# One decoder layer on one core: the branch, the masks, the gating and a modulation put elsewhere, and the first counts of two blocks held behind index sums

## The chip, the core and the metric

The kernel runs on one core of a Trainium2 chip. The metric is the device time of one execution in microseconds (us). Engines are named as the profile names them: PE (TensorE), PEld (its weight loads), DVE (VectorE), ACT (ScalarE), POOL (GpSimd), SP (SyncE).

## What is computed

One layer for 1024 positions of width 1024, in float32. The parts that this change touches, cut from the reference:

```python
# mixer A: spatial gating (4 groups of 128 channels, chunks of 128 positions)
z_u, z_v = gelu(p_u), gelu(p_v);  v = rms_norm(z_v per group)
out_A = u * (tril(W_s[g]) v_chunk + b[g])
# mixer B: sparse attention, 8 heads of 64; the indexer picks the 256 best keys of each query
dots  = einsum('bthd,bsd->bths', q_idx, k_idx) * IDX_DIM ** -0.5
score = einsum('bth,bths->bts', w * IDX_HEADS ** -0.5, relu(dots))      # causal
_, idx = top_k(score, 256)
o = softmax(q . k[idx] * HEAD_DIM ** -0.5) v[idx]
# then
x  = x + g1 * rms_norm(concat(rms_norm(out_A), rms_norm(o)) W_out)
h2 = rms_norm(x) * (1 + scale2) + shift2
x  = x + g2 * rms_norm(relu(h2 W_1)^2 W_2)
```

## The kernel before

The 1024 positions are eight blocks of 128 rows; block b has 128(b+1) causal keys, so only blocks 2 to 7 have keys to drop. A scheduler places all work: it walks the program in priority order (the order of the code, or a number set in `tc.cur_priority`), and fixes for each engine one list of instructions, which the engine then runs strictly in order. Semaphores between engines follow from the tiles; a tile with one buffer makes its users take turns.

The stages around the change:

- **Indexer (stage 3)**, blocks 7, 6, 5, 4, 3, 2. For each of 8 heads PE multiplies (L449) into PSUM tiles `lg`, ACT evicts with a relu (L450) into one of two `relu` buffers, and DVE adds them up into `SC` (L452 for the first head, L454 for the other seven). `qs` (L391/L392) are the stacked queries of the products.
- **Gating (stage 4)**, 16 block halves. PE projects u and v (24 matmuls, L301/L303/L304), ACT does gelu (L517), two squares (L522) and two scalings (L527), PE the gating product (L531), DVE adds the bias and multiplies (L534), ACT squares the result (L536). All of it stands in one function, `gating`, which is called one projection later. Then q of eight blocks is projected (`q_proj`, 24 matmuls each, copied by ACT, L560): six before the selection, two more in `search_rest`.
- **Selection (stage 5)**, blocks 7 to 2. `select` counts the positive scores (`count`, L592), prepares a 16-bit key (L622 to L627), and finds the threshold in 15 rounds: on DVE (blocks 7, 5, 2: L599, L601, L603, scratch `spare`) or on ACT by Sign (blocks 6, 4, 3: L611, with L612 and L613 on DVE, scratch `spare2`); a tail (L633 to L642) follows. `spare` and `spare2` have one buffer each, so searches on one engine take turns.
- **The branch**: `search_rest` brings a count from DVE through a PE product (L648), a cast (L649) and a load of the value into DVE's control flow (L652), which decides whether a longer search is run. It is not run with these inputs.
- **Masks**: `mask` (L667 to L680, DVE) turns threshold and scores of a block into a bias of its logits. `mask(7)` follows `search_rest` at once, the others are spread over the attention loop.
- **Attention (stage 6)**, blocks in the order 0, 7, 1, 6, 5, 4, 3, 2, four units each. Per unit: logits on PE (L727), evicted by DVE with the bias and a running extreme (L728), Exp on ACT (L731), transposes and values on PE (L766, L752).
- **Second norm (stage 8)**: `h2_block` transposes on PE (L895) and ACT evicts with the modulation (L898), 64 pieces of 128x128.

The order of masks 6 to 2 in the attention loop is set by `MASKS`, unit number to block:

```python
    MASKS = {4: 6, 6: 5, 8: 4, 9: 3, 10: 2}
```

Of the kernel before, what the change touches and what calls it, by code (L numbers as in the profile page):

```python
# [9 lines left out]
F32 = mybir.dt.float32  # L10
F32R = mybir.dt.float32r
BF = mybir.dt.bfloat16
# [7 lines left out]
P = 128  # L20
# [17 lines left out]
def trunk(ctx, tc, x, c, positions, w_ada, b_ada, g_pre_mix, w_in, g_sgu_v, w_spatial, b_spatial,  # L38
# [8 lines left out]
    def nm(s):  # L47
        uid[0] += 1
        return f"{s}_{uid[0]}"
# [16 lines left out]
    def p_tr():  # L66
        return ps.tile([P, 512], F32, tag="tr", name=nm("tr"), bufs=3)
# [354 lines left out]
                        pattern=[[-1, P]], channel_multiplier=1)  # L422
    i_stack, ip = push("ip", "right")
    stage(3)
    spare = up.tile([P, 1024], BF, name="spare")
    wC0 = w_chunk(w_in, [(0, C_QI, 512)])
    QI = {}
    IB = (7, 6, 5, 4, 3, 2)
# [1 line left out]
    def qi_proj(b):  # L430
        p = p_mm()
        proj(p, b, wC0, 512)
        QI[b] = ip.tile([P, 512], F32, tag="qi", name=nm("qi"), bufs=2)
        A.activation(QI[b], p, AF.Copy)
        rope(QI[b], b, 8, kp)

    def index(b):
        n = P * (b + 1)
        sc = SC[:, soff[b]:soff[b] + n]
        ch = chunks(n)  # L440
        for grp in range(2):
            qs = q_stack(ip, QI[b], grp, ip.tile([P, 2, 512], F32R, tag="qs", name=nm("qs"), bufs=2))
            for h4 in range(4):
                h = grp * 4 + h4
                r = ip.tile([P, 1024], F32, tag="relu", name=nm("relu"), bufs=2)
                for c0, w in ch:
                    pl = p_lg()
                    for q in range(2):
                        T.matmul(pl[:, :w], qs[:, q, h4 * P:(h4 + 1) * P], KI[:, c0:c0 + w], start=q == 0, stop=q == 1)  # L449
                    A.activation(r[:, c0:c0 + w], pl[:, :w], AF.Relu)  # L450
                if h == 0:
                    V.tensor_scalar(sc, r[:, :n], WI[:, b, h:h + 1], None, op0=OP.mult)  # L452
                else:
                    V.scalar_tensor_tensor(sc, r[:, :n], WI[:, b, h:h + 1], sc, op0=OP.mult, op1=OP.add)  # L454
        G.affine_select(out=sc[:, n - P:], in_=sc[:, n - P:], compare_op=OP.is_ge, fill=NEG, base=0,
                        pattern=[[-1, P]], channel_multiplier=1)

# [54 lines left out]
    stage(4)  # L512
    ssv = ct([P, NB, 4], F32, "ssv")
    ssa = ct([P, NB, 2], F32, "ssa")
    def gating(cc, j, p):
        uv = up.tile([P, 512], F32, tag="uv", name=nm("uv"), bufs=2)
        ge = A.activation(uv, p, AF.Gelu_apprx_tanh)  # L517
        vn = up.tile([P, 2, P], F32, tag="vn", name=nm("vn"), bufs=2)
        ss = ssv[:, j, 2 * cc:2 * cc + 2]
        v = uv[:, 256:512]  # L520
        for i in range(2):
            A.activation(vn[:, i], v[:, i * P:(i + 1) * P], AF.Square, accum_out=ss[:, i:i + 1])  # L522
        G.tensor_tensor(v, v, gvb[:, 256 * cc:256 * cc + 256], op=OP.mult)
        G.tensor_scalar(ss, ss, 1.0 / P, EPS, op0=OP.mult, op1=OP.add)
        G.tensor_tensor(ss, ss, mhalf[:, :2], op=OP.pow)
        for i in range(2):
            A.activation(vn[:, i], v[:, i * P:(i + 1) * P], AF.Copy, scale=ss[:, i:i + 1])  # L527
        pg = p_tr()
        ya = up.tile([P, 2, P], F32, tag="ya", name=nm("ya"), bufs=2)
        for i in range(2):  # L530
            T.matmul(pg[:, i * P:(i + 1) * P], WM[:, 2 * cc + i], vn[:, i], start=True, stop=True)  # L531
        for i in range(2):
            g = 2 * cc + i
            V.scalar_tensor_tensor(ya[:, i], pg[:, i * P:(i + 1) * P], cols[:, 72 + g:73 + g],  # L534
                                   uv[:, i * P:(i + 1) * P], op0=OP.add, op1=OP.mult)
        A.activation(vn.rearrange("p a b -> p (a b)"), ya.rearrange("p a b -> p (a b)"), AF.Square,  # L536
                     accum_out=ssa[:, j, cc:cc + 1])
        nc.sync.dma_start(ya_dram[j * P:(j + 1) * P, 256 * cc:256 * cc + 256], ya.rearrange("p a b -> p (a b)"))
        return ge

    pend = []
    for cc in range(2):
        wt = w_chunk(w_in, [(0, C_U + 256 * cc, 256), (256, C_V + 256 * cc, 256)])
        for j in range(NB):
            p = p_mm()
            proj(p, j, wt, 512)
            pend.append((cc, j, p))
            if len(pend) > 1:
                gating(*pend.pop(0))


    wQ = w_chunk(w_in, [(0, C_Q, 512)])
# [7 lines left out]
        A.activation(QT[b], p, AF.Copy)  # L560
        rope(QT[b], b, 8, qp)

    for b in OB[:6]:
        q_proj(b)
        if pend:
            last_gelu = gating(*pend.pop(0))

# [5 lines left out]
        G.memset(nth[:, k:k + 1], float(k + 1))  # L575
    spare2 = up.tile([P, 7 * P], mybir.dt.int8, name="spare2")
    ON_ACT = (6, 4, 3)

    ST = {}
    KDS = ct([P, 6], F32, "kds")  # L580
# [8 lines left out]
        return SC[:, soff[b]:soff[b] + P * (b + 1)]  # L589

    def count(b, thr, dst):
        V.tensor_scalar(BI[:, boff[b]:boff[b] + P * (b + 1)], score(b), thr, None, op0=OP.is_ge, op1=OP.add, accum_out=dst)  # L592

    def search(u, top, tf, cnt, kd, kk, step=lambda: None):

# [20 lines left out]
    def select(b):  # L616
        n = P * (b + 1)
        cnt, sg, kk, tf, kq, lf, top8, kd, th, lo, hi = ST[b]
        sc = score(b)
        jb = BI[:, boff[b]:boff[b] + n]  # L620
        count(b, 0.0, cnt)
        V.tensor_scalar(sg, cnt, TOPK - 0.5, 2.0, op0=OP.is_ge, op1=OP.mult)  # L622
        V.tensor_scalar(sg, sg, 1.0, None, op0=OP.subtract)
        a = (2 * TOPK - 1 - n) / 2.0
        V.tensor_scalar(kd, sg, a, n - TOPK + 1 + a, op0=OP.mult, op1=OP.add)

        V.tensor_scalar(jb, sc.bitcast(BF).rearrange("p (n two) -> p n two", two=2)[:, :, 1], sg, None, op0=OP.mult)  # L627
        u = jb.bitcast(I16)
        if b in ON_ACT:
            search_signs(u, 14, tf, cnt, kd, kk, kq)  # L630
        else:
            search(u, 14, tf, cnt, kd, kk)
        V.tensor_copy(hi, tf)  # L633
        V.tensor_scalar(spare[:, :n], u, tf, None, op0=OP.is_gt, op1=OP.add, accum_out=cnt)
        V.tensor_tensor(kd, kd, cnt, op=OP.subtract)

        V.scalar_tensor_tensor(jb.bitcast(U16), u, tf, sc.bitcast(U16).rearrange("p (n two) -> p n two", two=2)[:, :, 0],
                               op0=OP.is_equal, op1=OP.mult)
        v = jb.bitcast(U16)
        V.max(out=top8, in_=v)  # L640
        V.tensor_scalar(pick, nth, kd, None, op0=OP.is_equal)
        V.tensor_tensor_reduce(pick, pick, top8, scale=1.0, scalar=0.0, op0=OP.mult, op1=OP.add, accum_out=lf)  # L642

    def search_rest():

        V.tensor_scalar(more[:, :6], KDS, 8.0, None, op0=OP.is_gt, op1=OP.add, accum_out=more[:, 6:7])
        p = p_tr()
        flag = T.matmul(p[:1, :1], more[:, 6:7], ones, start=True, stop=True)  # L648
        V.tensor_copy(rest, p[:1, :1])  # L649
        for b in OB[6:]:  # L650
            q_proj(b, flag)
        with tc.tile_critical():  # L652
            r = V.value_load(rest)
            with V.If(r > 0):
                for b in range(2, NB):
                    cnt, sg, kk, tf, kq, lf, top8, kd, th, lo, hi = ST[b]
                    search(BI[:, boff[b]:boff[b] + P * (b + 1)].bitcast(U16), 15, lf, cnt, kd, kk, V.drain)
                V.drain()

    masked = [None]  # L660

    def mask(b):

# [1 line left out]
        cnt, sg, kk, tf, kq, lf, top8, kd, th, lo, hi = ST[b]  # L665
        sc = score(b)
        first = V.tensor_copy(lo, lf)  # L667
        V.scalar_tensor_tensor(th, hi, 16, lo, op0=OP.logical_shift_left, op1=OP.bitwise_or)

        V.tensor_tensor(tf, th.bitcast(F32), sg, op=OP.mult)  # L670
        lt = BI[:, boff[b]:boff[b] + n]
        eq = up.tile([P, 1024], BF, tag="uv", name=nm("eq"), bufs=2)[:, :n]
        after(first, masked[0])
        V.tensor_scalar(lt, sc, tf, None, op0=OP.is_lt, op1=OP.add, accum_out=cnt)
        V.tensor_scalar(eq, sc, tf, BIG, op0=OP.is_equal, op1=OP.mult)
# [6 lines left out]
    for b, pri in PRI:  # L682
        tc.cur_priority = pri
        select(b)
    tc.cur_priority = 465000
    search_rest()
    mask(7)


    stage(6)  # L690
# [24 lines left out]
    def logits(u):  # L715
# [3 lines left out]
        for h2 in range(2):  # L719
# [4 lines left out]
            for i, (c0, cw) in enumerate(ch):  # L724
                pl = p_lg()[:, :cw]
                for q in range(2):
                    T.matmul(pl, QS[b, grp][:, q, h4 * P:(h4 + 1) * P], KS[:, grp, c0:c0 + cw], start=q == 0, stop=q == 1)  # L727
                V.tensor_tensor_reduce(L[:, c0:c0 + cw], pl, bias[:, c0:c0 + cw], scale=-0.125, scalar=top,  # L728
                                       op0=OP.add, op1=OP.min, accum_out=mxs[:, i, b, h:h + 1])
                top = mxs[:, i, b, h:h + 1]  # L730
            ex = A.activation(L, L, AF.Exp, scale=-1.0, bias=top, accum_out=sms[:, b, h:h + 1])  # L731
# [94 lines left out]
    logits(0)  # L826
    stack_for(2)
    for u, (b, grp, pair) in enumerate(units):
        if u + 1 < len(units):
            logits(u + 1)  # L830
        values(u)
# [52 lines left out]
    def h2_block(j, y):  # L884
# [5 lines left out]
        for half in range(2):  # L890
# [4 lines left out]
                T.transpose(p[:, i * P:(i + 1) * P], y[:, k * P:(k + 1) * P], ident)  # L895
            for i in range(4):
                k = half * 4 + i
                A.activation(f[:, k, :], p[:, i * P:(i + 1) * P], AF.Identity, scale=G2[:, k:k + 1],  # L898
                             bias=SH2[:, k:k + 1])
        tk = slice(t, t + P)  # L900
        if hh == 0:
            for half in range(2):
# [379 lines left out]
```

## Time and profile before

| what | value |
|---|---|
| runs | 1244.34, 1246.61, 1664.87 us; median 1246.61 |
| profiled execution | 1243.53 us, of which the span of the profile is 1241.8 (1.7 outside it) |
| PE busy | 1161.0 us, 93% of the span |
| DVE busy | 861.9 us, 69% |
| ACT busy | 680.6 us, 55% |
| POOL busy | 212.0 us, 17% |
| chain that ended last | PE 59%, DVE 6%, issue 3%, ACT 3%, DMA 2% |

Busy shares are averages over stages with different limits; what a change in one stage is worth is read in that stage. A timeline row gives start and duration, the engine, the line, the operation, output <- input, and in brackets how long the engine had been idle before it and what ended that.

### The profile page before, as it was taken

How to read it: one execution, taken by the hardware profiler on the slowest of the kernel's cores; microseconds unless marked ns; L12 is line 12 of the kernel's file. 1: busy time of each engine (PE TensorE's matmuls, PEld its weight loads, DVE VectorE, ACT ScalarE, POOL GpSimd, SP SyncE). 2: the span in 40 equal slices, each digit the busy share in tenths (PEclk: the TensorE clock that was granted, in tenths of full speed). 3: DMA queues.
4: the chain of work that ended last, by engine and by line, in shares of the span. 5: the costliest groups of instructions: out<-in, count | busy, mean ns of one | idle time of the engine just before them, and what ended most of it. 6: DMA issues, size and time to landing. Idle time of an engine off the chain costs nothing.

```text
span 1241.8 us, 16873 instructions
## 1 busy us (share of the span) xinstructions
PE 1161.0 (93%) x5785; PEld 979.4 (79%) x5785; DVE 861.9 (69%) x1766; ACT 680.6 (55%) x1442; POOL 212.0 (17%) x304
## 2 busy tenths in 40 slices
PE   4899969899698999899899999999999999999997
PEld 4887857688588998887777888888887888888886
DVE  6944998956697666626698775655548756876568
ACT  4554569681267755538925555555544554445452
POOL 3695503553300000022510000000000000000001
PEclk9899969899799999999999999999999999999999
DMA  9431100210002044446315853444458455533335
GB/s 345 150 93 35 52 1 18 86 47 31 1 10 69 26 162 162 179 157 215 103 51 186 297 171 127 170 138 150 161 210 340 136 186 178 196 91 96 102 101 204
DMA packets 80240, 162.42 MB, mean 131 GB/s; under 512 B 7724, under 2 KB 32920, under 8 KB 80152
## 3 DMA queue, kind: packets, MB, share of 16 engines
q1 hardware_dynamic: 80136, 161.33, 38.6%
q8 instruction: 45, 0.74, 0.2%
q14 instruction: 43, 0.35, 0.1%
q10 hardware_dynamic: 16, 0.00, 0.0%
HBM read 119.36 MB, written 41.94 MB: 130 GB/s over the span
## 4 chain that ended last, share of the span: by engine, by line
PE 59%; DVE 6%; issue 3%; ACT 3%; DMA 2%; POOL 0%; SPq 0%; DVEq 0%; POOLq 0%; ACTq 0%
PE tr L1162 8%; PE lg L1162 8%; PE mm L1162 5%; PE mm L752 4%; PE lg L980 3%; PE lg L981 3%; PE lg L979 3%; PE tr L981 3%; PE tr L980 3%; PE tr L979 3%; PE tr L766 2%; PE lg L727 2%; PE mm L981 2%; PE mm L980 2%; PE mm L979 2%
## 5 line engine op out<-in xcount | busy, mean ns | idle before, releaser
L872 ACT ACTIVATE w<-rx 128x512 fp32r<-128x512 f32 x112 | 70.6, 631 | 146.4 <-PE lg L1162 61.7
L1162 PE MATMUL tr<-w,w 128*128 128x512 f32 x504 | 133.4, 389 | 2.7 <-DVE w L873 2.7
L1162 PE MATMUL lg<-w,w 128*128 128x512 f32 x504 | 133.1, 389 | 0.0
L873 DVE TENSOR_TENSOR w<-rx,w 128x512 fp32r<-128x512 f32 x112 | 77.2, 689 | 57.5 <-ACT w L872 57.3
L301 PE MATMUL mm<-w,hT 128*128 128x512 f32 (+1 forms) x288 | 112.0, 390 | 4.4 <-ACT hT L293 3.7
L1162 PEld LDWEIGHTS tr<-w,w 128*128 128x128 f32 x504 | 94.5, 188 | 22.7 <-DVE w L873 3.1
L303 PE MATMUL mm<-w,hT 128*128 128x512 f32 (+1 forms) x288 | 111.3, 387 | 0.0
L304 PE MATMUL mm<-w,hT 128*128 128x512 f32 (+1 forms) x288 | 110.3, 384 | 0.4 <-POOL hT L294 0.4
L1162 PEld LDWEIGHTS lg<-w,w 128*128 128x128 f32 x504 | 94.6, 188 | 19.6
L1198 POOL TENSOR_TENSOR rsf<-rsf,mhalf 128x1 f32<-128x1 f32 x8 | 6.0, 750 | 602.5 <-DVE rsf L1197 602.5
L1162 PE MATMUL mm<-w,w 128*128 128x512 f32 x336 | 93.9, 389 | 0.0
L752 PEld LDWEIGHTS mm<-VV,pT 128*128 128x128 f32 x576 | 73.4, 194 | 4.9 <-ACT pT L747 2.9
L752 PE MATMUL mm<-VV,pT 128*128 128x64 f32 x576 | 74.7, 273 | 1.3 <-ACT pT L747 1.3
L1162 PEld LDWEIGHTS mm<-w,w 128*128 128x128 f32 x336 | 63.1, 188 | 13.1
L873 DVE TENSOR_TENSOR w<-b,w 128x512 fp32r<-128x512 f32 x96 | 65.7, 685 | 3.8 <-ACT w L872 3.8
L301 PEld LDWEIGHTS mm<-w,hT 128*128 128x128 f32 x288 | 55.2, 192 | 15.1 <-ACT hT L293 3.9
L873 DVE TENSOR_TENSOR w<-s,w 128x512 fp32r<-128x512 f32 x56 | 38.1, 689 | 37.4 <-ACT w L872 37.4
L727 PE MATMUL lg<-KS,qs 128*128 128x512 f32 (+5 forms) x192 | 51.4, 376 | 12.6 <-DVE qs L392 10.7
L872 ACT ACTIVATE w<-b 128x512 fp32r<-128x512 f32 x96 | 59.3, 618 | 6.5 <-DMA b<-in_w_ff_dram 6.5
L304 PEld LDWEIGHTS mm<-w,hT 128*128 128x128 f32 x288 | 54.9, 191 | 10.0 <-POOL hT L294 0.6
L303 PEld LDWEIGHTS mm<-w,hT 128*128 128x128 f32 x288 | 55.3, 192 | 8.5
L731 ACT ACTIVATE L<-L,mxs 128x128 f32<-128x128 f32 (+7 forms) x64 | 49.2, 770 | 22.9 <-DVE mxs L728 22.7
(355 smaller groups left out, 2975.5 us busy)
## 6 DMA issues: line engine op xcount, KB each, us to landing
rx<-x_scratch SPq DMA_DIRECT2D x56, 512.0 KB, 3.6
x_scratch<-d SPq DMA_DIRECT2D x108, 256.0 KB, 3.0
ada<-in_w_ada_dram SPq DMA_DIRECT2D x48, 512.0 KB, 5.6
raw<-in_w_ff_dram SPq DMA_DIRECT2D x32, 512.0 KB, 4.0
b<-in_w_ff_dram SPq DMA_DIRECT2D x32, 512.0 KB, 4.4
x<-in_x_dram SPq DMA_DIRECT2D x16, 512.0 KB, 5.4
raw<-in_w_in_dram SPq DMA_DIRECT2D x8, 512.0 KB, 3.8
raw<-in_w_in_dram SPq DMA_DIRECT2D x16, 256.0 KB, 2.8
```

Of the source, the lines that this page charges most:

```text
L301: mm = T.matmul(p[:, :n], lh, wt[k][:, 0, :n], start=k == 0, stop=False)
L303: T.matmul(p[:, :n], lh, wt[k][:, 1, :n], start=False, stop=False)
L304: T.matmul(p[:, :n], ll, wt[k][:, 0, :n], start=False, stop=k == KD - 1)
L727: T.matmul(pl, QS[b, grp][:, q, h4 * P:(h4 + 1) * P], KS[:, grp, c0:c0 + cw], start=q == 0, stop=q == 1)
L731: ex = A.activation(L, L, AF.Exp, scale=-1.0, bias=top, accum_out=sms[:, b, h:h + 1])
L752: mm = T.matmul(po[:, o:o + 64], e[:, (si * 2 + h2) * P:(si * 2 + h2 + 1) * P], VV[:, s0 + si, grp], start=first, stop=pair == 1 and s0 + ...
L872: A.activation(hi, src, AF.Copy)
L873: eng.tensor_tensor(lo, src, hi.bitcast(F32), op=OP.subtract)
L979: ms.append(T.matmul(p, a[:, 0, k], b[:, 0, k], start=start and k == 0, stop=False, skip_group_check=more))
L980: ms.append(T.matmul(p, a[:, 0, k], b[:, 1, k], start=False, stop=False, skip_group_check=more))
L981: ms.append(T.matmul(p, a[:, 1, k], b[:, 0, k], start=False, stop=stop and k == 3, skip_group_check=more))
L1162: ms.append(T.matmul(p, x[:, qa, t * P:(t + 1) * P], y[:, qb], start=start and n == 0, stop=stop and n == 2, skip_group_check=more))
```

## The change

Seven edits, the diff cut to its core:

```diff
-    spare = up.tile([P, 1024], BF, name="spare")
+    spare = up.tile([P, 1024], mybir.dt.int8, name="spare")
...
+    summed = {}
...
-                    V.scalar_tensor_tensor(sc, r[:, :n], WI[:, b, h:h + 1], sc, op0=OP.mult, op1=OP.add)
+                    summed[b] = V.scalar_tensor_tensor(sc, r[:, :n], WI[:, b, h:h + 1], sc, op0=OP.mult, op1=OP.add)
...
-    def gating(cc, j, p):
-        uv = up.tile([P, 512], F32, tag="uv", name=nm("uv"), bufs=2)
+    def gate_in(cc, j, p):
+
+        uv = up.tile([P, 512], F32, tag="uv", name=nm("uv"), bufs=3)
...
+        pend.append((cc, j, uv, vn))
+        return ge
+
+    def gate_out(cc, j, uv, vn):
+
         pg = p_tr()
-        ya = up.tile([P, 2, P], F32, tag="ya", name=nm("ya"), bufs=2)
+        ya = up.tile([P, 2, P], F32, tag="ya", name=nm("ya"), bufs=1)
...
-        A.activation(vn.rearrange("p a b -> p (a b)"), ya.rearrange("p a b -> p (a b)"), AF.Square,
-                     accum_out=ssa[:, j, cc:cc + 1])
+        A.activation(pg[:, :2 * P], ya.rearrange("p a b -> p (a b)"), AF.Square, accum_out=ssa[:, j, cc:cc + 1])
...
-            pend.append((cc, j, p))
             if len(pend) > 1:
-                gating(*pend.pop(0))
+                gate_out(*pend.pop(0))
+            last_gelu = gate_in(cc, j, p)
...
-    for b in OB[:6]:
+    for b in OB[:4]:
         q_proj(b)
         if pend:
-            last_gelu = gating(*pend.pop(0))
+            gate_out(*pend.pop(0))
...
+    BEHIND = {7: 6, 6: 5}
...
-        count(b, 0.0, cnt)
+        after(count(b, 0.0, cnt), summed[BEHIND.get(b, b)])
...
-        for b in OB[6:]:
+        for b in OB[4:]:
             q_proj(b, flag)
...
+        if b < 7:
+            after(first, lowest[0])
...
-        eq = up.tile([P, 1024], BF, tag="uv", name=nm("eq"), bufs=2)[:, :n]
+        eq = up.tile([P, 1024], BF, tag="uv", name=nm("eq"), bufs=3)[:, :n]
...
-    tc.cur_priority = 465000
-    search_rest()
-    mask(7)
...
-                V.tensor_tensor_reduce(L[:, c0:c0 + cw], pl, bias[:, c0:c0 + cw], scale=-0.125, scalar=top,
+                lowest[0] = V.tensor_tensor_reduce(L[:, c0:c0 + cw], pl, bias[:, c0:c0 + cw], scale=-0.125, scalar=top,
...
     for u, (b, grp, pair) in enumerate(units):
+        if u == 3:
+            at = tc.cur_priority
+            tc.cur_priority = 465000
+            search_rest()
+            mask(7)
+            tc.cur_priority = at
...
-                A.activation(f[:, k, :], p[:, i * P:(i + 1) * P], AF.Identity, scale=G2[:, k:k + 1],
-                             bias=SH2[:, k:k + 1])
+                g, sh = G2[:, k:k + 1], SH2[:, k:k + 1]
+                if half == 0:
+                    A.activation(f[:, k, :], p[:, i * P:(i + 1) * P], AF.Identity, scale=g, bias=sh)
+                else:
+                    V.tensor_scalar(f[:, k, :], p[:, i * P:(i + 1) * P], g, sh, op0=OP.mult, op1=OP.add)
```

In words: (1) the first count of block 7 stands behind the last index sum of block 6, that of block 6 behind the last sum of block 5. (2) `gating` is split: gelu, squares and scaling right behind their own projection, the product and what follows one projection later; `uv` has three buffers, `ya` one, and the square of `ya` goes to PSUM. (3) Four q projections stand ahead of the selection, four in `search_rest`. (4) `search_rest` and `mask(7)` are emitted in the attention loop behind block 0's first units. (5) Masks of blocks below 7 stand behind the last logits eviction emitted. (6) `spare` holds 8-bit integers. (7) Half of the 64 modulations go from ACT to DVE. Behind the change lines shift by 2 to 17: L592 is L600, L599 L608, L611 L620, L627 L636, L648 L657, L728 L736.

Where DVE's list has the first count of block 7 (`self_2716` before, `self_2650` in the changed kernel; 128x1024 is block 7, 128x896 block 6). Before:

```order
L392 TENSOR_TENSOR qs_1221<-tr_1224,qs_1221 128x512
L592 TENSOR_SCALAR BI,self_2716<-SC 128x1024
L452 TENSOR_SCALAR SC<-relu_1181,WI 128x896
L622 TENSOR_SCALAR self_2716<-self_2716 128x1
L454 SCALAR_TENSOR_TENSOR SC<-relu_1191,WI,SC 128x896
L623 TENSOR_SCALAR self_2716<-self_2716 128x1
L625 TENSOR_SCALAR kds<-self_2716 128x1
L627 TENSOR_SCALAR BI<-SC,self_2716 128x1024
L454 SCALAR_TENSOR_TENSOR SC<-relu_1201,WI,SC 128x896
L599 TENSOR_SCALAR spare,self_2716<-BI,self_2716 128x1024
```

In the changed kernel:

```order
L456 SCALAR_TENSOR_TENSOR SC<-relu_1231,WI,SC 128x896
L456 SCALAR_TENSOR_TENSOR SC<-relu_1241,WI,SC 128x896
L456 SCALAR_TENSOR_TENSOR SC<-relu_1251,WI,SC 128x896
L456 SCALAR_TENSOR_TENSOR SC<-relu_1261,WI,SC 128x896
L600 TENSOR_SCALAR BI,self_2650<-SC 128x1024
L392 TENSOR_TENSOR qs_1357<-tr_1360,qs_1357 128x512
L631 TENSOR_SCALAR self_2650<-self_2650 128x1
L632 TENSOR_SCALAR self_2650<-self_2650 128x1
L634 TENSOR_SCALAR kds<-self_2650 128x1
L636 TENSOR_SCALAR BI<-SC,self_2650 128x1024
L454 TENSOR_SCALAR SC<-relu_1317,WI 128x768
L608 TENSOR_SCALAR spare,self_2650<-BI,self_2650 128x1024
```

The count and the first round (L599, L608) of block 7 stood among the first sums of block 6 (`relu_1181` and on); now all eight sums of block 6 are ahead of them, and the rounds stand among the sums of block 5 (`relu_1317` and on).

Where ACT's list has the first Sign of block 6 (`self_2714` before, `self_2648` in the changed kernel; relus of 128x384 belong to block 5, of 128x320 to block 4). Before:

```order
L391 ACTIVATE qs_1357<-tr_1360 128x512
L450 ACTIVATE relu_1317<-lg_1318 128x384
L450 ACTIVATE relu_1317<-lg_1322 128x384
L450 ACTIVATE relu_1327<-lg_1328 128x384
L611 ACTIVATE spare_2701,self_2714<-BI,self_2714 128x896
L450 ACTIVATE relu_1327<-lg_1332 128x384
L611 ACTIVATE spare_2701,self_2714<-BI,self_2714 128x896
```

In the changed kernel:

```order
L391 ACTIVATE qs_1546<-tr_1549 128x512
L452 ACTIVATE relu_1483<-lg_1484 128x320
L452 ACTIVATE relu_1483<-lg_1488 128x320
L452 ACTIVATE relu_1503<-lg_1504 128x320
L452 ACTIVATE relu_1503<-lg_1508 128x320
L620 ACTIVATE spare_2635,self_2648<-BI,self_2648 128x896
L452 ACTIVATE relu_1513<-lg_1514 128x320
L452 ACTIVATE relu_1513<-lg_1518 128x320
```

It stood among the relus of block 5's second head; now it stands behind those of block 4's fifth head.

Where PE's list has the flag of the branch (`ones,more`), with projections of q behind it (`mm`) and logits of blocks 0 and 7 (`lg`, 128x128 and 128x512). Before:

```order
L304 MATMUL mm_2659<-w_2470,hT_143 128x512
L301 MATMUL mm_2659<-w_2473,hT_143 128x512
L303 MATMUL mm_2659<-w_2473,hT_143 128x512
L304 MATMUL mm_2659<-w_2473,hT_143 128x512
L648 MATMUL tr_3073<-ones,more 1x1
L301 MATMUL mm_3076<-w_2446,hT_142 128x512
L303 MATMUL mm_3076<-w_2446,hT_142 128x512
```

In the changed kernel:

```order
L760 MATMUL mm_3056<-VV,pT_3079 128x64 x2
L735 MATMUL lg_3869<-KS,qs_3086 128x512
L735 MATMUL lg_3873<-KS,qs_3086 128x512
L735 MATMUL lg_3879<-KS,qs_3086 128x512
L760 MATMUL mm_3108<-VV,pT_3112 128x64 x2
L735 MATMUL lg_3869<-KS,qs_3086 128x512
L735 MATMUL lg_3873<-KS,qs_3086 128x512
L735 MATMUL lg_3879<-KS,qs_3086 128x512
L714 MATMUL tr_3123<-ident,ya_3116 128x128 x4
L657 MATMUL tr_3131<-ones,more 1x1
L301 MATMUL mm_3134<-w_2448,hT_143 128x512
L303 MATMUL mm_3134<-w_2448,hT_143 128x512
```

Before, the sixth q projection was right ahead of the flag and all logits behind it; now the logits of block 0 and the first three of block 7 stand ahead of it. Behind it come four q projections instead of two, the last two of them ahead of the logits that end the second of block 7's four units.

## Rows read from the trace of the kernel before

**Rows 1.** Waits of PE, 100 to 400 us: total, times, longest.

```profile
PE lg L727 <- DVE qs L392: 10.7, 1, 10.7
PE lg L449 <- ACT relu L450: 10.1, 8, 2.6
PE tr L531 <- ACT vn L527: 5.0, 1, 5.0
```

**Rows 2.** Windows: length, busy of each engine, granted clock, DMA share, GB/s.

```profile
core 0: us, PE busy (x) PEld busy (x) DVE busy (x) ACT busy (x) POOL busy (x), PEclk, DMA share, GB/s
147.00:190.00 43.00, 32.88 (x122) 25.37 (x121) 42.00 (x104) 26.71 (x60) 2.97 (x6) 0.72 0.00 1
147.00:302.40 155.40, 139.18 (x604) 113.34 (x603) 133.19 (x426) 102.62 (x290) 55.87 (x87) 0.89 0.12 36
302.40:342.40 40.00, 28.19 (x136) 23.47 (x134) 22.36 (x54) 9.66 (x27) 11.55 (x19) 0.83 0.00 1
342.40:386.00 43.60, 38.97 (x307) 35.14 (x306) 40.23 (x114) 32.45 (x70) 3.67 (x6) 1.00 0.16 49
560.00:640.00 80.00, 72.22 (x330) 58.32 (x329) 56.23 (x89) 59.48 (x131) 29.47 (x26) 0.96 0.38 131
```

**Rows 3.** DVE timeline: end of the last search, the branch, masks 7 and 6, block 7's evictions.

```profile
302.40 0.08 DVE L642 DVE_READ_ACCUMULATOR2_ANT self<- 128x1 f32 x1
310.36 0.15 DVE L649 CAST rest<-tr 1x1 int32<-1x1 f32 x1 [7.87 <-PE tr L648]
319.54 0.15 DVE L667 CAST seli<-self 128x1 int32<-128x1 f32 x1 [9.04 <-DVEq L652]
...
327.94 0.14 DVE L667 CAST seli<-self 128x1 int32<-128x1 f32 x1
...
334.23 1.08 DVE L680 SCALAR_TENSOR_TENSOR BI<-BI,eq 128x896 bf16<-128x896 bf16 x1
...
342.41 0.68 DVE L728 CUSTOM_DVE_ANT_0 L<-lg,BI 128x512 f32<-128x512 f32 x1
...
350.85 0.75 DVE L728 CUSTOM_DVE_ANT_0 L<-lg,BI,mxs 128x512 f32<-128x512 f32 x1
```

**Rows 4.** DVE timeline, counts of blocks 7 and 6 and block 6's last sum.

```profile
125.05 1.22 DVE L592 TENSOR_SCALAR_CACHE_REDUCE BI<-SC 128x1024 bf16<-128x1024 f32 x1
150.53 1.14 DVE L454 SCALAR_TENSOR_TENSOR SC<-relu,WI,SC 128x896 f32<-128x896 f32 x1
153.45 1.08 DVE L592 TENSOR_SCALAR_CACHE_REDUCE BI<-SC 128x896 bf16<-128x896 f32 x1
```

**Rows 5.** ACT timeline: block 6's last relu, first and last Sign, a q copy.

```profile
145.89 0.52 ACT L450 ACTIVATE relu<-lg 128x448 f32<-128x448 f32 x1
...
157.34 1.04 ACT L611 ACTIVATE spare<-BI,self 128x896 int8<-128x896 int16 x1 [5.08 <-DVE BI L627]
...
278.39 0.72 ACT L611 ACTIVATE spare<-BI,self 128x512 int8<-128x512 int16 x1 [0.65 <-DVE self L613]
...
299.36 0.60 ACT L560 ACTIVATE q<-mm 128x512 f32<-128x512 f32 x1 [4.84 <-PE mm L304]
```

**Rows 6.** Groups on DVE by shape, 100 to 330 us: busy, mean ns, idle before.

```profile
L599 DVE TENSOR_SCALAR_CACHE_REDUCE spare<-BI,self 128x1024 bf16<-128x1024 int16 x15 | 19.1, 1276 | 0.3
L603 DVE SCALAR_TENSOR_TENSOR self<-self 128x1 f32<-128x1 f32 x45 | 11.9, 264 | 0.8
L454 DVE SCALAR_TENSOR_TENSOR SC<-relu,WI,SC 128x1024 f32<-128x1024 f32 x7 | 10.8, 1539 | 8.1 <-ACT relu L450 7.8
L534 DVE SCALAR_TENSOR_TENSOR ya<-tr,cols,uv 128x128 f32<-128x128 f32 x32 | 9.8, 345 | 4.2 <-PE tr L531 4.2
L601 DVE TENSOR_SCALAR self<-self,kds 128x1 f32<-128x1 f32 x45 | 9.4, 210 | 0.9
L454 DVE SCALAR_TENSOR_TENSOR SC<-relu,WI,SC 128x768 f32<-128x768 f32 x7 | 7.4, 1063 | 0.0
```

**Rows 7.** The modulation: its group on ACT, and PE's wait for it, 540 to 640 us.

```profile
L898 ACT ACTIVATE x<-tr,SH,G 128x128 f32<-128x128 f32 x64 | 24.0, 492 | 0.8 <-PE tr L895 0.8
...
PE tr L895 <- ACT x L898: 2.2, 2, 1.3
PE tr L979 <- ACT x L898: 1.3, 1, 1.3
```

More of the change, by code (lines that the diff above doesn't have):

```diff
@@ L535, in gating @@
                                    uv[:, i * P:(i + 1) * P], op0=OP.add, op1=OP.mult)
-        A.activation(vn.rearrange("p a b -> p (a b)"), ya.rearrange("p a b -> p (a b)"), AF.Square,
-                     accum_out=ssa[:, j, cc:cc + 1])
+        A.activation(pg[:, :2 * P], ya.rearrange("p a b -> p (a b)"), AF.Square, accum_out=ssa[:, j, cc:cc + 1])
         nc.sync.dma_start(ya_dram[j * P:(j + 1) * P, 256 * cc:256 * cc + 256], ya.rearrange("p a b -> p (a b)"))
-        return ge
     pend = []
@@ L591, in count @@
     def count(b, thr, dst):
-        V.tensor_scalar(BI[:, boff[b]:boff[b] + P * (b + 1)], score(b), thr, None, op0=OP.is_ge, op1=OP.add, accum_out=dst)
+        return V.tensor_scalar(BI[:, boff[b]:boff[b] + P * (b + 1)], score(b), thr, None, op0=OP.is_ge, op1=OP.add,
+                               accum_out=dst)
     def search(u, top, tf, cnt, kd, kk, step=lambda: None):
@@ L658, in search_rest @@
                 V.drain()
-    masked = [None]
+    masked, lowest = [None], [None]
     def mask(b):
```

## The prediction

> **What bounds the kernel now.** I read the page's shares first: PE is busy 93% of the span and carries 59% of the chain that ended last, so an edit pays only where it takes idle or slow time from PE, and costs only where it adds some. So next came PE's waits in the stretch that the change touches [rows 1]: 10.1 us for relus of the indexer (eight waits), 5.0 for a scaled v of the gating, 10.7 for stacked queries at the start of the attention. Then the windows [rows 2]: from 147 to 190 us PE is busy 32.88 of 43.00 at a granted clock of 0.72, while DVE is busy 42.00. DVE has too much to do there: block 7's search and block 5's index sums share it, relus wait for buffers that sums have not freed, and PE waits for relus. From 302.4 to 342.4 PE is busy 28.19 of 40 (clock 0.83). That is the branch: DVE ends the last search at 302.48, gets the flag at 310.4 because PE reaches the flag's product only then, and starts mask 7 at 319.54 [rows 3]. Behind it, from 342.4 to 386, DVE (40.23 of 43.60) and PE (38.97) are both nearly full.
>
> So the time hangs on two things: how early the chain of searches ends (F, 302.4 now), and what PE still has to do between F and the first eviction of block 7, which needs mask 7 (T7, 342.41 now).
>
> **The hold on the first counts.** Before, DVE counts block 7 at 125.05 and runs eight of its rounds before block 6's last sum at 150.53 [rows 4]. With the hold it has only sums to do, and the sums of block 6 come as fast as the relus: the last relu ends at 146.4 [rows 5], its sum near 147.6. That is 4 us earlier than 151.7. But count 7 (1.22, [rows 4]) and its rounds, each 1.276 + 0.210 + 0.264 and 0.08 to read the result, 1.83 us [rows 6], move behind it. By the order, block 6's first Sign now stands behind: count 7 and its preparation (2.4), block 5's eight sums (7 x 1.063 + 0.61, 8.1, [rows 6]), three stackings of queries (2.1), six rounds of 7 (11.0), count 6 (1.1), and four sums of block 4 with a round and small ones (7.5). 147.6 + 32.2 makes 180, against 157.34 [rows 5]: 22 us later. Nothing shows that this frees PE: rounds stood between sums before, and they stand there still, now between those of block 5.
>
> **How late F becomes.** Two workings. (a) By the chain: 45 Signs of blocks 6, 4, 3 take turns on one scratch, 157.34 to 278.39, and the tail of 3 and the search of 2 last to 302.4. That is 145 us from first Sign to F; the same from 180 gives 325. (b) By DVE's load: between 147 and 302.4 it works 133.2 us [rows 2]. The deferred part of search 7 adds 2.4 + 8 x 1.83 = 17, two sums of 6 leave (2.4), and block 0's evictions, which now come ahead of the flag, bring some 6.6 (22.36 busy in 302.4 to 342.4, less masks 7 and 6, which take from 319.54 to 335.31). That is 154 us: F = 302 if DVE never idles, 327 at the 86% of before (133.2 of 155.4), 305 at the 98% of 147 to 190. I take 322, between (a) and the middle of (b), and keep 302 and 335; the upper end is the chain with 10 us more, since Signs of block 3 now stand in ACT's list behind q copies and block 0's Exps, which wait for PE.
>
> **Four q projections instead of six.** PE is done with the fourth by 299.4 [rows 5], or some 5 us earlier if the gating stall is gone, and spends a few us on block 0's logits. Then it waits for the flag, 20 us or more where it now has none: PE's work is shifted from ahead of F to behind F. From F to the masks nothing shortens: flag and cast 0.4, the branch 9.04, mask 7 8.4 [rows 3]. T7 = 322 + 18 = 340, two us earlier than now. But of the four projections behind the flag (5.44 each, the spacing of the q copies, one of them in [rows 5]), two stand ahead of block 7's fourth logits, which wait for a PSUM bank until T7, and two behind: PE does the second pair only then. Block 7's eighth eviction, at 350.85 now, comes at 340 + 0.7 + 2 + 10.9 + 1.5 = 355: **4 us later**.
>
> **Masks.** Mask 6 (327.94 to 335.31, 7.4 us, [rows 3]) was done while PE waited anyway, and mask 5 in between as well. Both now stand behind block 7's first eight evictions: 7.4 and, by width, 6.3, so 13.7 us more for a DVE that had 3.4 idle in the next 43.6 [rows 2]. Some of it is covered by attention stages behind, where PE has work of its own. Without cover it is all 13.7, with full cover nothing; I take half, **7 us**.
>
> **Gating split, buffers, 8-bit scratch.** PE's 5.0 of [rows 1] go, and with them slow clock around it, but PE now waits for the flag, so this lies ahead of a wait and I count nothing; at most 5. The third `uv` and the single `ya` move no instruction of the sum. The 8-bit scratch: L599 writes 16 bit and takes 1276 ns for 1024 elements [rows 6], which is already more than 1 ns an element; I count nothing. As an upper bound the 128x1024 sum with 32-bit output costs 1539 [rows 6], 0.26 more per count, 12 us for 45.
> The Trainium skill, "VectorE: DVE Perf Modes", section "The perf-mode tier table", gives `tensor_scalar` with 16-bit operands in SBUF its fastest mode, 4x (693 ns for 2048 elements), and asks 16 bit of every tensor: by it an 8-bit output would give up a fast mode that the counts had. An estimate from that page is 0.35 us for 1024 elements; this case's trace disagrees, with 1.276 us at 16 bit, so for these counts there is no such mode to lose.
>
> **Modulation.** 32 of 64 pieces leave ACT (492 ns each, [rows 7]: 12 us) and come to DVE. The nearest DVE row is a 128x128 product out of PSUM, 345 ns [rows 6]: 11 us, over 23.8 idle us of DVE in 560 to 640 [rows 2]. PE's waits for the modulation are 2.2 and 1.3 [rows 7], and 7.8 is all its idle time there. I take **3 us gained**; bounds: 7.8 gained, 3 lost, if each block's four pieces (1.4 us) stand ahead of something that PE waits for twice.
>
> **The sum.** 1243.53 (profiled) + 4 + 7 - 3 = 1251.5. The median shown is 3.1 above the profiled execution, the faster run 0.8; I add 1.5 and say **1253**.
>
> **The rivals.**
> 1. *The searches do not end late* (faster): freed from gating stalls, ACT and DVE run at the 98% of 147 to 190, and F lies at 302 to 310. For it: (b) allows it. Against it: the first Sign is late by 22 us, and the searches take turns. T7 is then 320 to 328, and the sum -16 to -8, +7, -3: 1231 to 1239, on the median's scale 1233 to 1242.
> 2. *DVE becomes the bound behind the branch* (slower): F at 335 as above, and masks 6 and 5 find no cover. Place: between T7 and block 6's first logits. Price: +17 + 13.7 - 3 = 28, 1271; with a cover of half and F at 330, 1262. It decides from F above 328 or so. For it: DVE at 40.23 of 43.60 [rows 2]. Against it: PE has projections to fill time with.
> 3. *The stall only moves* (no change): F's delay is just what PE gains by running ahead, the masks are covered: 1244 to 1247.
> 4. *The 8-bit scratch slows the counts*: the 12 us above in the chain, 1265. Against it: [rows 6].
>
> **How the numbers follow.** Likeliest, 1246 to 1262 with 1253 as its middle: 0.52. Rival 1: 0.22. Rival 2: 0.17. Rival 3: 0.06. Rival 4: 0.03. The range must leave out no more than 2 in 10: from the middle of rival 1, 1236, to beyond the middle of rival 2, 1272, the likeliest alone being 1246 to 1262. About 2% is what a measurement of this kernel tells from no change: 1222 and 1271. Rival 1 falls below 1222 only if the modulation and the gating bring their bounds as well: 0.05. Slower by over 2% is about half of rival 2 and a little of rival 4: 0.10. Within 2%: 0.85.
>
> **What would show it.** In the changed profile: block 6's last sum near 147 and count 7 right behind; first Sign near 180; the tail of the last search near 322; PE idle some 20 us ahead of the flag, where the projections stood; 9 us of branch; the first 512-wide eviction near 340; PE busy with projections while DVE waits behind it, then mask 6 at 355; half the modulation on DVE with fewer PE waits. It is wrong if the last search ends before 312 (rival 1), or if PE waits for mask 6 before block 6's logits by more than 10 us (rival 2).

## The result, and the profile after

The changed kernel takes 1261.68 us in the median (1259.35 to 1266.86), the kernel before 1245.57: a ratio of 1.0133, interval 1.011 to 1.0156. It is slower by 16 us, clearly beyond its interval but within 2%. The ratio leaves out the execution of 1664.87 us of the kernel before. The forecast of 1253 had the direction, and the time lies inside the range, but the forecast rise over the kernel before was 7 us, and 16 were measured.

Waits of PE from 100 to 420 us in the changed kernel (line, what it waited for, total, times, longest), which answer to [rows 1]:

```profile
PE tr L657 <- DVE more L655: 18.8, 1, 18.8
PE lg L451 <- ACT relu L452: 6.4, 9, 2.0
PE lg L735 <- DVE mxs L736: 5.8, 3, 5.2
PE lg L735 <- ACT qs L391: 5.1, 1, 5.1
...
PE tr L539 <- ACT vn L530: 1.7, 1, 1.7
```

The gating stall of 5.0 is down to 1.7, the relu waits from 10.1 to 6.4, and one wait of 18.8 us for the flag of the branch has come, with 5.2 for the first evictions of block 7 behind it.

The windows of the changed kernel (columns as in [rows 2]):

```profile
147.00:190.00 43.00, 36.62 (x165) 28.95 (x164) 41.04 (x91) 24.68 (x63) 4.64 (x9) 0.92 0.01 4
147.00:302.40 155.40, 140.37 (x645) 115.72 (x644) 132.75 (x401) 111.37 (x315) 58.43 (x90) 0.93 0.12 36
302.40:342.40 40.00, 15.91 (x62) 12.32 (x61) 27.31 (x94) 1.36 (x3) 2.00 (x5) 0.71 0.03 8
342.40:386.00 43.60, 43.60 (x299) 39.90 (x299) 29.17 (x78) 25.50 (x51) 6.19 (x15) 0.94 0.03 7
560.00:640.00 80.00, 72.67 (x340) 59.88 (x338) 57.35 (x109) 52.49 (x107) 32.67 (x29) 0.96 0.47 162
```

From 147 to 190 PE is better off: 36.6 us busy instead of 32.9, at a clock of 0.92 instead of 0.72. From 302.4 to 342.4 it is much worse off: 15.9 instead of 28.2. DVE, nearly full from 342.4 to 386 before, now idles there (29.2 of 43.6) while PE does projections.

The timeline of the changed kernel at the places of [rows 3] to [rows 5] (DVE, ACT and PE rows, in order of time):

```profile
147.41 1.15 DVE L456 SCALAR_TENSOR_TENSOR SC<-relu,WI,SC 128x896 f32<-128x896 f32 x1 [2.04 <-ACT relu L452]
148.48 1.21 DVE L600 TENSOR_SCALAR_CACHE_REDUCE BI<-SC 128x1024 bf16<-128x1024 f32 x1
...
177.89 1.04 ACT L620 ACTIVATE spare<-BI,self 128x896 int8<-128x896 int16 x1 [1.07 <-DVE BI L636]
...
300.35 0.72 ACT L620 ACTIVATE spare<-BI,self 128x512 int8<-128x512 int16 x1 [0.54 <-DVE self L622]
...
322.27 0.19 PE L657 MATMUL tr<-ones,more 128*1 128x1 f32 x2 [18.84 <-DVE more L655]
...
322.73 0.08 DVE L651 DVE_READ_ACCUMULATOR2_ANT self<- 128x1 f32 x1
333.68 0.16 DVE L676 CAST seli<-self 128x1 int32<-128x1 f32 x1 [10.87 <-DVEq L661]
...
341.34 0.69 DVE L736 CUSTOM_DVE_ANT_0 L<-lg,BI 128x512 f32<-128x512 f32 x1
...
342.10 0.79 PE L735 MATMUL lg<-KS,qs 128*128 128x512 f32 x1 [5.22 <-DVE mxs L736]
...
358.51 0.69 DVE L736 CUSTOM_DVE_ANT_0 L<-lg,BI 128x512 f32<-128x512 f32 x1 [3.72 <-PE lg L735]
...
359.36 0.75 DVE L736 CUSTOM_DVE_ANT_0 L<-lg,BI,mxs 128x512 f32<-128x512 f32 x1
360.03 0.15 DVE L676 CAST seli<-self 128x1 int32<-128x1 f32 x1
...
397.80 0.62 DVE L736 CUSTOM_DVE_ANT_0 L<-lg,BI 128x448 f32<-128x448 f32 x1
```

Count 7 now follows the last sum of 6 directly, block 6's first Sign is at 177.9 (157.3 before), and the last search (its tail ends in L651) ends at 322.8 instead of 302.5. The eighth eviction of block 7 starts at 359.36 instead of 350.85, and only then does mask 6 start, at 360.03 instead of 327.94.

Where the 16 us arise, by the start of the same instruction in both profiles:

| landmark | before | after | later by |
|---|---|---|---|
| block 6's first Sign (ACT) | 157.34 | 177.89 | 20.6 |
| product of the flag (PE) | 310.13 | 322.27 | 12.1 |
| block 7's first eviction | 342.41 | 341.34 | -1.1 |
| block 7's eighth eviction | 350.85 | 359.36 | 8.5 |
| block 6's first eviction | 386.43 | 397.80 | 11.4 |
| first output projection | 432.56 | 448.31 | 15.8 |
| first product of the feed-forward part | 594.73 | 610.74 | 16.0 |
| first product of the last stage | 926.05 | 941.16 | 15.1 |
| last product | 1230.98 | 1249.05 | 18.1 |

All of it has come by the first output projection. The 3 us at the very end are no part of it: the stretch from the last stage's first product to its last took 304.9 us in the kernel before, 307.9 in the changed one, and 303.9 to 309.3 in the variants below, all with the same code there.

### The profile page after: what moved, and what is told of

Same layout as the page of the kernel before. It is cut to its first block, busy times and chain, and to the rows that moved or that the text cites. A ratio compares the mean times of both kernels' runs of the same rounds, so it can differ in the third digit from the quotient of the medians.

```text
span 1259.9 us, 16892 instructions
## 1 busy us (share of the span) xinstructions
PE 1166.4 (93%) x5785; PEld 986.2 (78%) x5785; DVE 873.7 (69%) x1798; ACT 671.4 (53%) x1410; POOL 211.6 (17%) x304
## 4 chain that ended last, share of the span: by engine, by line
PE 52%; DVE 10%; DMA 4%; issue 3%; ACT 2%; POOL 1%; SPq 0%; DVEq 0%; POOLq 0%; ACTq 0%
PE tr L1179 8%; PE lg L1179 8%; PE mm L1179 5%; PE mm L760 4%; PE lg L996 2%; PE lg L997 2%; PE lg L998 2%; PE lg L735 2%; PE tr L774 2%; PE tr L997 2%; PE tr L998 2%; PE tr L996 2%; DVE w L887 2%; PE mm L996 2%; PE mm L998 2%
## 5 line engine op out<-in xcount | busy, mean ns | idle before, releaser
L760 PEld LDWEIGHTS mm<-VV,pT 128*128 128x128 f32 x576 | 76.4, 200 | 5.9 <-ACT pT L755 3.8
L735 PE MATMUL lg<-KS,qs 128*128 128x512 f32 (+5 forms) x192 | 55.4, 401 | 11.0 <-DVE mxs L736 5.8
L456 DVE SCALAR_TENSOR_TENSOR SC<-relu,WI,SC 128x1024 f32<-128x1024 f32 (+5 forms) x42 | 45.7, 1088 | 20.1 <-ACT relu L452 19.4
```

What stands on the lines that cost most here:

```text
L456: summed[b] = V.scalar_tensor_tensor(sc, r[:, :n], WI[:, b, h:h + 1], sc, op0=OP.mult, op1=OP.add)
L760: mm = T.matmul(po[:, o:o + 64], e[:, (si * 2 + h2) * P:(si * 2 + h2 + 1) * P], VV[:, s0 + si, grp], start=first, stop=pair == 1 and s0 + ...
```

## The experiments

Theory A: the holds put off the chain of searches that ends in the flag; PE runs dry ahead of the flag and has more work behind it. The rivals: the new places of branch, masks and projections cost by themselves (B), the late masks (C), the modulation on DVE (D).

**The holds undone**

```diff
-    BEHIND = {7: 6, 6: 5}
+    BEHIND = {}
```

> The changed kernel with one part undone: the first counts of blocks 7 and 6 are no longer held behind the sums of the next block (each stands behind the last sum of its own). Theory A: the hold puts off the searches of 7 and 6, and so the end of the last search, by 20 us; PE runs dry ahead of the flag. Then here the first Sign of 6 is back near 158 us (177.9 in the changed kernel), the last search ends near 304 (322.8), the first 512-wide eviction is near 324 (341.3), and the time is 1245 us (1243 to 1249, 1261.7 for the changed kernel). Rival B: the new places of the branch, the masks and two q projections cost it by themselves, wherever the searches end: 1256 or more, with the first Sign early all the same.

Measured: 1246.43 us, ratio to the kernel before 0.9999 (0.9984 to 1.0014). The first Sign is at 156.2, PE's wait for the flag is 10.6, block 7's first eviction at 328.8. Nearly the whole rise is gone with the two holds; rival B would have left it at 1256. The flag's cast came at 310.0, six us later than I expected: the evictions of block 0 now stand among the rounds of the last search. So about 8 of the 20 us by which the last search ends late in the changed kernel (310.3 here, 302.5 before) are there without any hold.

**Six q projections ahead of the flag, holds kept**

```diff
-    for b in OB[:4]:
+    for b in OB[:6]:
...
-        for b in OB[4:]:
+        for b in OB[6:]:
```

> The changed kernel with the q projections split as before, six ahead of the selection and two behind the flag. Theory A: the last search ends at 322 as in the changed kernel, PE's wait for the flag falls from 18.8 to about 8 us, and the two projections that stood ahead of block 7's last logits of its second unit are gone: block 7's eighth eviction comes 9 to 12 us earlier (359.4 in the changed kernel, 348 to 350 here), and the time is 1251 us (1249 to 1254). Rival: DVE with its five masks is the bound behind the branch, so an earlier eviction is given back: 1258 to 1262.

Measured: 1249.15 us, ratio 1.0031 (1.0011 to 1.005). The wait for the flag is 12.3 us, and the eighth eviction at 351.0, level with the kernel before, although the flag's product is at 325.8. The last search ended at 326.3, four us later than expected, and the wait was 12 us instead of 8. Either undone part takes back 12 to 15 of the 16 us. From these two runs alone that could be one price that is paid only when both parts are in, or two prices with a gain from the other edits beside them; the kernel with neither part, below, decides for the second.

**Masks free of the order behind the last eviction**

```diff
-        if b < 7:
-            after(first, lowest[0])
```

> The changed kernel without the order that puts the masks of blocks below 7 behind the last logits eviction; mask 6 then stands right behind mask 7, as before the change. Theory A: mask 6 (7.4 us) runs there while PE has q projections, but block 7's evictions come later by the same 7 us, so no change: 1261 us (1258 to 1264). Rival C: the late masks are what is paid (7 us of the 16): 1254 us (1252 to 1257), and block 6's first eviction 7 us earlier (397.8 in the changed kernel).

Measured: 1259.33 us, ratio 1.011 (1.008 to 1.014). The eighth eviction came at 363.9 (4.5 later), the first output projection at 448.2 (448.3): the masks cost the same time early or late. Rival C is out: it wanted block 6's first eviction 7 us earlier, and it came 4 us later (402.1).

**All modulation on ACT**

```diff
-                if half == 0:
+                if half >= 0:
```

> The changed kernel with all 64 modulations on ACT again. Theory A: the move of 32 to DVE gained 1 us between the start of the output projections and the first products of the feed-forward part (the lag against the kernel before fell from 16.1 to 15.1 us), so 1263 us here (1261 to 1265). Rival D: the 32 pieces cost time on DVE, 3 us that the changed kernel loses late: 1258 or less.

Measured: 1260.23 us, ratio 1.0109 (1.0081 to 1.0137); the interval overlaps that of the changed kernel. Neither the gain (3 us in the prediction, 1 us in the expectation) nor the loss of rival D is there. PE's waits from 555 to 660 us show why. With all pieces on ACT:

```profile
PE tr L909 <- ACT x L914: 2.2, 2, 1.3
PE mm L812 <- DVE x L947: 1.4, 1, 1.4
PE tr L909 <- ACT x L952: 1.4, 2, 1.0
PE tr L996 <- ACT x L914: 1.0, 1, 1.0
```

In the changed kernel:

```profile
PE tr L909 <- ACT x L952: 6.2, 1, 6.2
PE mm L812 <- DVE x L947: 1.2, 1, 1.2
```

The waits for the modulation (L914) went as forecast, and one wait of 6.2 us for the scaling of rows (L952, ahead of it in each block) came in their place. The trace of the changed kernel shows what held it up: DVE had the sum of squares ready for POOL at 627.5, POOL got to it at 629.8, behind 4.7 us of other work (L929 and L931), and ACT scaled the rows at 631.4. Whether DVE's share brought that order about was not tried.

**Which hold: block 7's alone, then block 6's alone**

```diff
-    BEHIND = {7: 6, 6: 5}
+    BEHIND = {7: 6}
```

> The changed kernel with the hold on block 7 alone (behind the last sum of 6); block 6's count is free again. Theory A1 (the chain of the Signs of 6, 4, 3 sets the end of the searches, so only the hold on 6 counts): first Sign of 6 at 153 to 160, last search ends at 308 to 313, 1247 us (1244 to 1250), as without any hold. Theory A2 (DVE's load sets it: the rounds of 7 that were put off have to be done somewhere): last search at 318 or later, 1258 us or more, wherever the first Sign stands.

```diff
-    BEHIND = {7: 6, 6: 5}
+    BEHIND = {6: 5}
```

> The changed kernel with the hold on block 6 alone (behind the last sum of 5); block 7 counts early again. Theory A1 (the chain): first Sign of 6 at 172 to 179, last search ends at 318 to 323, 1259 us (1256 to 1263), as in the changed kernel. Theory A2 (DVE's load): with the rounds of 7 in the early gaps again, the last search ends at 308 to 313, 1248 us.

Measured: 1246.29 us with the hold on 7 (ratio 1.0007, 0.9988 to 1.0025) and 1258.10 with the hold on 6 (1.0095, 1.0064 to 1.0127). First rows of Sign on ACT and ends of the last search on DVE, with the hold on 7, then with the hold on 6:

```profile
153.53 1.04 ACT L620 ACTIVATE spare<-BI,self 128x896 int8<-128x896 int16 x1 [1.27 <-DVE BI L636]
...
310.31 0.08 DVE L651 DVE_READ_ACCUMULATOR2_ANT self<- 128x1 f32 x1
```

```profile
178.15 1.04 ACT L620 ACTIVATE spare<-BI,self 128x896 int8<-128x896 int16 x1
...
317.16 0.08 DVE L651 DVE_READ_ACCUMULATOR2_ANT self<- 128x1 f32 x1
```

The rounds of 7 end at 216.7 with its hold and at 183.6 without, and by itself that costs nothing: the last search ends at 310.4, as without any hold (310.3), and DVE works 140.1 us between 147 and 302.4 instead of 133.4, so the late rounds went into time that it had idle. The hold on 6 delays the head of the chain 6, 4, 3 that takes turns on one scratch, and with it the end: A1 holds and A2 does not. The delay does not come through whole: 22 us at the first Sign (156.2 without holds) are 7 at the end of the last search (317.2, just short of A1's 318). Where 6 is held, the hold on 7 adds 5.6 us there (322.8 in the changed kernel) and 3.6 us in the time, which the intervals do not separate.

**The holds alone, in the kernel before**

```diff
+    summed = {}
...
-                    V.scalar_tensor_tensor(sc, r[:, :n], WI[:, b, h:h + 1], sc, op0=OP.mult, op1=OP.add)
+                    summed[b] = V.scalar_tensor_tensor(sc, r[:, :n], WI[:, b, h:h + 1], sc, op0=OP.mult, op1=OP.add)
...
-        count(b, 0.0, cnt)
+        after(count(b, 0.0, cnt), summed[{7: 6, 6: 5}.get(b, b)])
```

> The kernel before with both holds and nothing else. Theory A: first Sign near 178 (157.3 before), last search near 318 (302.4), PE waits 15 to 25 us for the flag behind its six q projections, first 512-wide eviction near 353 (342.4): 1256 us (1252 to 1260, 1245 for the kernel before). Rival: the hold alone is harmless, it only costs together with four q projections ahead of the flag: 1243 to 1249.

Measured: 1256.44 us, ratio 1.0084 (1.0056 to 1.0112). First Sign at 174.3, flag's cast at 314.6, first 512-wide eviction at 352.95. The holds need no other edit to cost 10 us. Six projections stand ahead of the flag here, so they cost also without the moved projections. PE's wait for the flag is 11.1 us, less than the 15 to 25 that I expected. A second wait, by the profile for a step of a mask (L679), stands where PE waited 10.7 us for stacked queries before [rows 1] (100 to 420 us):

```profile
PE lg L729 <- DVE self L679: 12.0, 1, 12.0
PE tr L650 <- DVE more L648: 11.1, 1, 11.1
```

**Neither hold, and six projections ahead of the flag**

```diff
-    BEHIND = {7: 6, 6: 5}
+    BEHIND = {}
...
-    for b in OB[:4]:
+    for b in OB[:6]:
...
-        for b in OB[4:]:
+        for b in OB[6:]:
```

> The changed kernel without the holds and with six q projections ahead of the flag; the split gating, the 8-bit scratch, the places of branch and masks and the modulation stay as changed. Theory A: each of the two undone parts took its own 12 to 15 us, and they overlap only in part: last search near 311, flag wait of PE under 5 us, first 512-wide eviction near 330 and the eighth near 337 (350.9 in the kernel before), 1237 us (1234 to 1242), faster than the kernel before. Rival: the late masks 6 and 5 take it back on DVE: 1244 to 1249.

Measured: 1232.29 us, ratio 0.9894 (0.9869 to 0.992): this beats both kernels. The two undone parts add up (15 and 13 us apart, 29 together), where I had thought that they overlap. So the 16 us of the change are a difference: its two bad parts cost 29, and its other edits bring 12 to 13. The flag, the end of the branch, and the first and eighth eviction on DVE:

```profile
308.82 0.13 DVE L658 CAST rest<-tr 1x1 int32<-1x1 f32 x1
...
317.96 0.15 DVE L676 CAST seli<-self 128x1 int32<-128x1 f32 x1 [8.85 <-DVEq L661]
...
325.63 0.69 DVE L736 CUSTOM_DVE_ANT_0 L<-lg,BI 128x512 f32<-128x512 f32 x1
...
332.61 0.75 DVE L736 CUSTOM_DVE_ANT_0 L<-lg,BI,mxs 128x512 f32<-128x512 f32 x1
```

The flag's cast is only 1.5 us earlier than in the kernel before (310.36, [rows 3]), but the first eviction is 16.8 us earlier. Block 0's logits and stacks are done ahead of the flag here; mask 6 stands behind block 7's evictions, but with it right behind mask 7 again (below, free masks) the first eviction is at 326.1, so the masks are not the reason.

**The split gating alone, in the kernel before**

```diff
-    spare = up.tile([P, 1024], BF, name="spare")
+    spare = up.tile([P, 1024], mybir.dt.int8, name="spare")
...
-    def gating(cc, j, p):
+    def gate_in(cc, j, p):
...
+    def gate_out(cc, j, uv, vn):
...
             if len(pend) > 1:
-                gating(*pend.pop(0))
+                gate_out(*pend.pop(0))
+            last_gelu = gate_in(cc, j, p)
```

> The kernel before with the split gating alone (with what it needs: three uv buffers, one ya buffer, the 8-bit scratch). Theory A: the searches end as before (302 to 306), PE reaches the flag some 6 us earlier since it no longer stalls on the gating (310.1 in the kernel before), the first 512-wide eviction moves from 342.4 to about 337, 1239 us (1236 to 1242, 1244.6 for the kernel before). Rival: the stall was hidden behind the branch and masks, and the searches get no earlier: 1243 to 1247; then the 12 us of the variant without holds and with six projections come from block 0's logits ahead of the flag and the later masks.

Measured: 1243.07 us, ratio 0.9987 (0.997 to 1.0004): no change, as the rival had it. The flag's product came at 301.2 instead of 310.1, 9 us earlier, and only 4 of them reached block 7's first eviction (338.3). PE's waits from 100 to 420 us:

```profile
PE lg L731 <- DVE qs L392: 11.8, 1, 11.8
PE tr L652 <- DVE more L650: 10.1, 1, 10.1
```

PE is faster through the gating and then waits for the flag, and again 11.8 us for the stacked queries, for which it waited 10.7 before [rows 1]. So the gain of the variant above is not from the split gating by itself. What is left is the new place of the branch, with block 0's logits and stacks ahead of the flag, alone or together with the split gating; it was not tried by itself.

**Hold on 7 with six projections; no holds, six projections and free masks**

The first of these kernels differs from the changed one by `BEHIND = {7: 6}` and the six projections, the second by `BEHIND = {}`, the six projections and masks without the order.

> The changed kernel with the hold on block 7 alone and six q projections ahead of the flag. Theory A: as without any hold, since the head of the chain is free: first Sign near 154, last search near 311, 1233 us (1229 to 1237). If the gaps that the hold leaves on DVE at 126 to 147 us cost anything: 1238 or more.

> The changed kernel without holds, with six q projections ahead of the flag, and without the order that puts masks 6 to 2 behind the last logits eviction. Theory A (masks cost DVE the same time early or late): block 7's first eviction 8 us later and the late stage 7 us shorter, 1233 us (1230 to 1237), the same as with the order (1232.3). Rival: the order is where the gain over the kernel before lies: 1240 or more.

Measured: 1235.95 us (0.9932, 0.9911 to 0.9952) and 1236.50 us (0.9925, 0.9901 to 0.995), both within what theory A gave. Neither beats 1232.29, and neither the hold on 7 nor the order of the masks is worth much either way: 4 us, with intervals that overlap.

## Why the prediction was right in its mechanism and short in size

Two terms of the sum failed. The stretch from the flag to block 7's eighth eviction was to be 4 us late and was 8.5, and the modulation was to gain 3 us and gained none.

- **The holds.** Right in place and size: last sum of 6 ends at 148.6 (147.6 forecast), first Sign at 177.9 (180). I did not separate the two holds; the runs show that the one on block 6 is the main price. The sentence that nothing here frees PE was wrong: with the holds alone PE was busy 36.2 us from 147 to 190 (32.9 before), and the copy of its sixth q projection began at 303.2 (310.2 before). In the changed kernel the fourth projection ended at 283.8, not near 295. The gain went into the wait for the flag, so the sum did not miss it.
- **The end of the searches.** Forecast 322, measured 322.8, and the closeness is in part luck. Of the two workings, the chain's is the one that the runs bear out (hold on 6 alone: late; hold on 7 alone: not). But it took the 145 us from first Sign to end as fixed. They are 145 in the changed kernel too, yet 139 with the hold on 6 alone and 157 with the hold on 7 alone; and some 8 of the 20 us of delay are there without the holds, with block 0's evictions among the last rounds, which only the other working, by DVE's load, had counted (6.6 us).
- **From the flag to the eighth eviction.** Forecast 4 us late, measured 8.5: this term was half of what it should be. Two things make it up. The branch took 10.87 us where I had copied 9.04, and with mask 7 at 7.7 instead of 8.4 the first eviction was at 341.3, not 340. And from there to the eighth eviction it took 18.0 us, not 15.1, since I costed PE at full clock behind its waits: up to the projections PE took 3.9 us instead of 2, and for the two projections 11.9 instead of 10.9. PE's windows in the changed kernel (columns as in [rows 2]):

```profile
303.40:322.30 18.90, 0.06 (x3) 0.06 (x2) 17.36 (x74) 0.00 (x0) 0.00 (x0) 0.59 0.06 14
322.30:330.50 8.20, 8.20 (x28) 6.53 (x29) 0.51 (x4) 0.01 (x1) 0.00 (x0) 0.69 0.00 0
337.00:342.10 5.10, 0.00 (x1) 0.00 (x1) 4.96 (x7) 0.00 (x0) 0.00 (x0) 0.90 0.00 0
342.10:346.00 3.90, 3.90 (x13) 3.22 (x13) 2.83 (x8) 2.04 (x4) 0.18 (x1) 0.50 0.00 0
346.00:358.00 12.00, 12.00 (x51) 9.87 (x50) 2.79 (x7) 3.74 (x8) 3.32 (x9) 0.92 0.00 1
```

  Behind the wait of 18.8 us the first 24 projection matmuls took 8.1 us instead of 5.7, at a granted clock of 0.69 over the stretch; that cost nothing, since PE then waited for the first eviction. Behind the wait of 5.2 us the clock was 0.50, the lower of its two levels (1.2 of 2.4 GHz), and 3.9 us of work at that clock would be some 2 at full clock. That, and a part of the next 12 us at 0.92, is what was missing. It is read from the trace; no run kept PE busy there to test it.
- **The masks.** Forecast 7 us, measured 7.2, from the eighth eviction to the first output projection (8.5 to 15.8). That they cost the same early or late was not said, and the run without their order shows it. How much of the 7.2 is theirs is not shown: in that run 4.5 us moved ahead of the eighth eviction, and 2.6 stayed behind it.
- **The modulation.** Forecast a gain of 3 us, measured none (1260.2 without it, 1261.7 with it). I took PE's waits for L898 as gone and did not ask what was late next: the scaling of the next rows.
- **Gating and 8-bit scratch.** Counted at nothing, and the run with these alone is level. My bound of 5 us was wrong all the same: with them alone the copy of the sixth q projection began at 291.2 instead of 310.2, 19 us earlier, and 10 of them went into the wait for the flag. The rival of slow 8-bit counts is out; in the changed kernel (100 to 330 us, as in [rows 6]) the count is as fast as with 16 bit:

```profile
L608 DVE TENSOR_SCALAR_CACHE_REDUCE spare<-BI,self 128x1024 int8<-128x1024 int16 x15 | 19.1, 1273 | 0.2
```

- **The sum.** 8.5 + 7.2 + 0 makes 15.7, where I had 4 + 7 - 3 and 1.5 for the scale of the median. Rival 2, which I gave 17 in 100, came near in time (1262) by another way: the searches ended at 322.8, not at 328 or later.

## What to carry to other kernels

Of several chains that take turns on a buffer each, find the one that the late result hangs on, and its head: holding back that head costs a good part of its delay (here 17 to 24 us at block 6's first Sign, 7 to 17 at the end of the last search, 10 to 17 in the time, in pairs of runs with and without the hold on it), while holding back the head of a chain with slack, as block 7 here, cost nothing by itself. Work that stands behind a late flag should be little, and work that needs no flag should stand ahead of it: here six projections and block 0's logits ahead of it, with the chain's head free and the other edits kept, took 12 us off the kernel before. And a wait that an edit creates can cost more than its length: here PE's granted clock was 0.50 for 3.9 us behind a wait of 5.2 us, while behind the wait of 18.8 us the slow matmuls cost nothing, since a further wait followed.

## What the runs showed of the hardware that I had not expected

DVE's idle time at the branch is not one number: it was 9.04 us in the kernel before, 8.85 with neither hold and six projections, and about 9.0 in the two other profiles in which PE hardly waited for the flag; in the nine profiles in which PE had waited 8 us or more, the changed kernel's among them, it was 10.4 to 11.4. Why it is longer there was not tried. The Trainium skill, "Advanced Engine Details and Errata", section "Control Flow Timing", gives about 108 ns for compare-and-branch. No run here shows the branch by itself; DVE's idle time around the load of the value and the branch is 80 to 105 times that.
